# One-hot rows of four tokens as two pairs, one reduction over index candidates, and a GpSimd subtraction in pieces, in a two-layer decoder trunk

## The chip, the cores and the metric

The kernel runs on one core of one Trainium2 chip. The metric is the time of one execution on the device in microseconds (us), as the median of several runs. A profile is one further execution of the same program, recorded by the hardware profiler. Engine names are those of the profile: PE is TensorE's matmul, PEld its weight load, DVE is VectorE, ACT is ScalarE, POOL is GpSimd, SP is SyncE, whose queue issues most loads.

## What is computed

The reference is a decoder trunk of two layers on 256 tokens of width 1024. Each layer is a pair of token mixers (a gated linear recurrence and a stick-breaking attention) and then a PEER feed-forward block, which is where the change lies:

```
q = (h @ w_pq).reshape(B, S, 8 heads, 2, 64)
s1, s2 = q[..., 0, :] . sub_keys[0], q[..., 1, :] . sub_keys[1]     # 128 scores each
v1, i1 = top_k(s1, 16);  v2, i2 = top_k(s2, 16)
cand     = v1[:, None] + v2[None, :]                                # 256 candidates
cand_idx = i1[:, None] * 128 + i2[None, :]
top, pos = top_k(cand, 16);  idx = take_along_axis(cand_idx, pos)
gates    = softmax(top)
out      = sum over (head, k) of gates * gelu(h . peer_u[idx]) * peer_v[idx]
```

There are 128 x 128 = 16,384 experts, 8 heads and 16 experts a head, so 128 chosen experts per token.

## The kernel before

The kernel does not gather rows of `peer_u`. It computes the products of all experts with all tokens, multiplies them by a matrix of gates that is zero except at the chosen experts, and multiplies the result by all of `peer_v`. Everything is float32 in accuracy: each matmul operand is split into a rounded half `wh` and a remainder `wl`, and three matmuls (high by high, high by low, low by high) make one product.

**Loads and their preparation.** A list `order` holds all weight loads in the order of their use. `fetch` (line 179) issues the next one on SP into one of five `raw` buffers. A load of `peer_u` is one tile of 128 x 1024 in four DMAs (line 191). `turn` (line 209) transposes a `peer_u` tile in 32 x 32 blocks on DVE (line 214, `raw<-raw`). `prep` (line 221) makes the halves of a tile in two steps of 512 columns: ACT copies `raw` into `wh` (through `act`, line 58), and the remainder `wl = raw - wh` is a subtraction (line 254). For `peer_u` it is GpSimd's, with the columns taken in an order of blocks (`p a k r`); for other weights DVE or GpSimd does it. `take` (line 285) hands over a prepared tile, issues the next load, prepares the next tile and transposes the one after.

**The stage of `peer_u`** (lines 1302 to 1630) goes over 128 tiles, 126 of them in one loop (line 1622). Each `u_tile` (line 1605) issues 24 matmuls of 256 columns into the bank `A`: all 256 tokens against one tile. Every second tile, `fin_u` (line 1592) applies the gelu (ACT, tile `gel`) and, where the gates of a token are already in place, multiplies on DVE (line 1600).

After each tile the loop calls `pull(sides, 1.55)` (line 618), which runs a generator of side work: every step yields a cost, `pull` goes on until the budget of the tile is spent, and `yield None` ends the work for this tile. So the code's order on each engine is fixed at build time by these costs. The side work is:

- `topk` (line 1338): the two top-16 searches of every head and token block on DVE, with a small matmul for the scores (bank `K`).
- its second part (lines 1429 to 1477), which turns positions into indices. For each of the two token blocks and the two key halves `a`, it compares 16 positions with 16 candidates (`m`, 8 heads x 16 x 16 = 2048 values of float16, line 1449), multiplies by the candidates' indices (line 1453), and adds over the 16 candidates by halving: 1024, 512, 256 values (line 1458) and a last addition of 128 (line 1460). Two transposes per block go to PE (line 1469).
- `place_gates` (line 1480): for each block `b` of `TB` = 4 tokens, `build` makes one-hot rows. `o` is 1 where a key number equals a chosen index (line 1486), for both key halves; `og` is the row of the second half times the gate, itself in two float16 halves (line 1488). Both are tiles `[128, 2, 128 keys, 4 tokens]` of float16, 1024 values a partition, with the token innermost. `prod` then makes the gates of each token as `o`'s first half times `og`, eight matmuls of 128 columns per block (bank `G`, line 1497), with the weights `o[:, 0, :, q]` and the moving columns `og[:, a, :, q]`. Both are read with a step of four values, that is 8 bytes. `put` copies `G` out (ACT, and DVE at line 1512). The matmuls of block `b - 1` are issued ahead of the building of block `b`, and the copies behind it. There are 64 blocks a layer.

On each engine the order in a tile with gates is therefore: PE 24 matmuls `A`, then 8 matmuls `G`; DVE the transpose of a later `peer_u` tile, every second tile the multiplication by the gelu, the two operations of `build`, the multiplications of `put`; POOL the two subtractions of the next tile, each behind ACT's copy; ACT the copies of `put`, which wait for `G`, then the copies `wh` of the next tile.

**The stage of `peer_v`** (lines 1691 to 1718) has no part in the change.

Of the kernel before, what the change touches and what calls it, by code (L numbers as in the profile page):

```python
# [8 lines left out]
F32 = mybir.dt.float32  # L9
F32R = mybir.dt.float32r  # L10
F16 = mybir.dt.float16
# [5 lines left out]
P = 128  # L17
# [28 lines left out]
def trunk_kernel(ctx: ExitStack, tc: tile.TileContext, x, c, w_ada, b_ada, w_in, lb_logits, hg_norm_g,  # L46
# [174 lines left out]
    def prep():  # L221


        turn(1)
        kind, t = fetched[0]
        kind = kind[0]
        if kind in "mk":
            fetched.popleft()
            prepped.append((kind, t, None, None))
            return True  # L230
        place = room_for(kind)
        if not place:
            return False
        fetched.popleft()
        live.append(place)
        hs, ls = [], []
        if kind == "v" and state.get("vprep"):
            state["vprep"]()
        for s in range(2):
            h = place.tile([P, 512], F32R, name="wh")  # L240
            lo = place.tile([P, 512], F32R, name="wl")
            hs.append(h)
            ls.append(lo)
            if kind == "u":
                src = t.rearrange("p (a k r) -> p a k r", a=4, k=KC)[:, :, 4 * s:4 * s + 4]
                h, lo = (a.rearrange("p (k a r) -> p a k r", k=4, a=4) for a in (h, lo))
            else:
                src = t[:, s * 512:(s + 1) * 512]
            act(h, src, AF.Copy)
            if kind == "u" or state.get("pool_lo"):  # L250
                eng = nc.vector if s and state.get("share_lo") else nc.gpsimd
            else:
                eng = lighter(0.6, 1.0) if kind == "o" or kind == "w" and not state.get("slab") else nc.vector
            eng.tensor_sub(lo, src, h.bitcast(F32))  # L254
        h, lo = halves(hs), halves(ls)
        prepped.append((kind, h, lo, place))
        return True
# [50 lines left out]
        return prepped[0][0] if prepped else fetched[0][0][0] if fetched else None  # L308


    iota_t = const.tile([P, NK, TB], F16, name="iota_t")
    iota_k = const.tile([P, TOPK, TOPK], F16, name="iota_k")
    nc.gpsimd.tensor_copy(iota_t, iota_f[:, :, None].to_broadcast([P, NK, TB]))
    nc.gpsimd.tensor_copy(iota_k, iota_f[:, :TOPK, None].to_broadcast([P, TOPK, TOPK]))
    cols = const.tile([P, P], F32, name="cols")
    lncols = const.tile([P, 2, DEPTH, 2, KC], F32, name="lncols")
# [985 lines left out]
    def peer(l, hT):  # L1302
        with ExitStack() as es:
# [8 lines left out]
            with ExitStack() as eu:  # L1312
# [13 lines left out]
                def per_head(a):  # L1326
                    return a.rearrange("p (h k) -> p h k", h=PH)
# [10 lines left out]
                def topk():  # L1338
# [90 lines left out]
                    for tt in range(2):  # L1429
# [14 lines left out]
                        for a in range(2):  # L1444
                            iv = per_head(half[2 + a])[:, :, :, None].to_broadcast(k4)
                            for q in range(0, PH, 4):
                                act(ix[:, q:q + 4], iv[:, q:q + 4], AF.Copy)
                                yield None
                            nc.vector.tensor_tensor(m, per_head(half[a])[:, :, None, :].to_broadcast(k4),
                                                    iota_k[:, None].to_broadcast(k4), op=OP.is_equal)  # L1450
                            yield 1.1
                            yield None
                            nc.vector.tensor_mul(m, m, ix)
                            yield 1.1
                            w = TOPK
                            while w > 2:
                                w //= 2
                                nc.vector.tensor_add(m[:, :, :w], m[:, :, :w], m[:, :, w:2 * w])  # L1458
                                yield 0.3
                            nc.vector.tensor_add(per_head(sel[a]), m[:, :, 0], m[:, :, 1])  # L1460
                            yield 0.2
                        nc.vector.tensor_reduce(sm[:, :PH], tp, axis=mybir.AxisListType.X, op=OP.add)
                        nc.vector.reciprocal(sm[:, :PH], sm[:, :PH])
                        nc.vector.tensor_mul(tp, tp, sm[:, :PH][:, :, None].to_broadcast([P, PH, TOPK]))
# [15 lines left out]
                def place_gates():  # L1480

                    def build(b):
                        bs = slice(b * TB, (b + 1) * TB)
                        o = up.tile([P, 2, NK, TB], F16, name="o2", bufs=2)
                        og = up.tile([P, 2, NK, TB], F16, name="o3", bufs=3)
                        nc.vector.tensor_tensor(o, iT[:, :, None, bs].to_broadcast([P, 2, NK, TB]),  # L1486
                                                iota_t[:, None].to_broadcast([P, 2, NK, TB]), op=OP.is_equal)
                        nc.vector.tensor_mul(og, gT[:, :, None, bs].to_broadcast([P, 2, NK, TB]),  # L1488
                                             o[:, 1:2].to_broadcast([P, 2, NK, TB]))
                        built[b] = o, og  # L1490

                    def prod(b):
                        pg = psk.tile([P, TB, NK], F32, name="G")
                        o, og = built.pop(b)
                        for q in range(TB):
                            for a in range(2):
                                mm(pg[:, q], o[:, 0, :, q], og[:, a, :, q], a == 0, a == 1)
                        return pg

                    def put(b, pg):  # L1500
                        jd = progress["j"]
                        ts = slice(b * TB, (b + 1) * TB)
                        i = jd // NB_J
                        if jd < NK:
                            act(buf[i][:, jd % NB_J:, ts], pg[:, :, jd:(i + 1) * NB_J].rearrange("p t j -> p j t"), AF.Copy)
                        for i2 in range(i + 1, NK // NB_J):
                            act(buf[i2][:, :, ts], pg[:, :, i2 * NB_J:(i2 + 1) * NB_J].rearrange("p t j -> p j t"), AF.Copy)
                        for i2 in range(0, min(i + 1, NK // NB_J)):
                            n = min(jd - i2 * NB_J, NB_J)
                            if n > 0:  # L1510
                                dst = buf[i2][:, :n, ts]
                                nc.vector.tensor_mul(dst, pg[:, :, i2 * NB_J:i2 * NB_J + n].rearrange("p t j -> p j t"), dst)
                        progress["t"] = (b + 1) * TB

                    built, prods = {}, {}
                    nb = S // TB
                    for b in range(nb + 1):
                        if 0 <= b - 1 < nb:
                            prods[b - 1] = prod(b - 1)
                        if b < nb:  # L1520
                            build(b)
                        yield 1.2
                        if 0 <= b - 1 < nb:
                            put(b - 1, prods.pop(b - 1))

                        yield 0.1 + 0.2 * progress["j"] / NB_J
                        yield None
# [238 lines left out]
```

## Time and profile before

| | us |
|---|---|
| median of 3 runs | 2266.94 |
| the 3 runs | 2264.68, 2266.94, 2272.71 |
| the profiled execution, own time | 2268.03 |
| its span, first to last instruction | 2266.3 |
| granted TensorE clock, mean of the profiled execution | 0.979 |
| `peer_u` stage of layer 0, first to last | about 320 to 785 |
| `peer_u` stage of layer 1 | about 1435 to 1897 |

Start times are counted from the span's start. A group's row in the profile reads: line, engine, operation, output<-inputs, shapes, xcount | busy us, mean ns of one | idle time just before them and what ended it. "Busy" includes the time in which an instruction has been started and is held up. A row of the windows view reads: window, its length, then busy time and instruction count for PE, PEld, DVE, ACT and POOL, the granted clock, the DMA share and GB/s. A row of the chain of waits or of the timeline begins with start and length in us.

### The profile page before, as it was taken

The page shows a single profiled execution, that of the slowest core. Times are in us where ns is not written, and L with a number is a line of the kernel's source. Part 1 is how long each engine was busy: PE and PEld are TensorE (multiplying, and loading weights), DVE is VectorE, ACT ScalarE, POOL GpSimd, SP SyncE. Part 2 cuts the span into 40 slices and gives each one's busy share as a digit, 9 for nine tenths or more (in the row PEclk, how much of TensorE's full clock was granted, in tenths as well). Part 3 has the DMA queues.
Part 4 walks back from the last instruction along what each step waited for, and adds up shares of the span by engine and source line. Part 5 has one row for each costly group of instructions (what it writes and reads, how often), then busy time and mean ns, then how long its engine had stood idle before and what let it go on. Part 6 is the DMA issues. An engine that isn't in the chain of part 4 may idle for free.

```text
span 2266.3 us, 41171 instructions
## 1 busy us (share of the span) xinstructions
PE 2142.0 (95%) x14084; PEld 1951.7 (86%) x14084; DVE 1899.3 (84%) x3480; ACT 1116.2 (49%) x2347; POOL 1047.4 (46%) x760
## 2 busy tenths in 40 slices
PE   5789899899999999999989998998999999999998
PEld 5789799889999978888779897998999998788886
DVE  7877989999999878888887558999999997666675
ACT  3446544544444454555545564445444445455562
POOL 4656648786777610000045534687767773200001
PEclk8999999999999999999999999999999999999999
DMA  8546556555555578888844335564555555666672
GB/s 280 187 139 224 156 142 172 147 135 144 141 142 139 159 251 263 284 280 287 291 136 149 112 123 139 156 170 133 139 141 143 144 139 176 203 194 193 195 224 92
DMA packets 269515, 400.24 MB, mean 177 GB/s; under 512 B 29776, under 2 KB 216696, under 8 KB 269304
## 3 DMA queue, kind: packets, MB, share of 16 engines
q1 hardware_dynamic: 267560, 392.33, 57.3%
q0 software_dynamic: 1408, 4.23, 0.5%
q8 instruction: 110, 1.80, 0.3%
q10 hardware_dynamic: 336, 1.06, 0.1%
q14 instruction: 101, 0.83, 0.1%
HBM read 396.46 MB, written 1.05 MB: 175 GB/s over the span
## 4 chain that ended last, share of the span: by engine, by line
PE 70%; DVE 14%; DMA 5%; issue 4%; POOL 3%; ACT 2%; SPq 1%; POOLq 0%; DVEq 0%; ACTq 0%
PE Y L61 27%; PE A L61 25%; PE T L61 7%; PE G L61 6%; POOL wl L254 3%; DMA raw<-in_peer_u_dram 3%; PE hs L61 2%; PE ss L61 2%; DVE wl L254 2%; SPq L191 1%; DVE qk L840 1%; DVE e L826 1%; DMA raw<-in_peer_v_dram 1%; DVE mh L364 1%; DVE buf L1458 1%
## 5 line engine op out<-in xcount | busy, mean ns | idle before, releaser
L254 POOL TENSOR_TENSOR wl<-raw,wh 128x512 fp32r<-128x512 f32 x663 | 918.9, 1410 | 707.8 <-ACT wh L58 642.5
L58 ACT ACTIVATE wh<-raw 128x512 fp32r<-128x512 f32 x1188 | 682.7, 622 | 206.8 <-PE A L61 48.0
L61 PE MATMUL A<-hTh,wh 128*128 128x256 f32 x2080 | 545.3, 294 | 8.4 <-ACT wh L58 8.4
L61 PE MATMUL A<-hTl,wh 128*128 128x256 f32 x2080 | 528.0, 286 | 0.0
L61 PE MATMUL Y<-wh,o 128*128 128x512 f32 x1776 | 479.9, 392 | 0.1
L254 DVE TENSOR_TENSOR wl<-raw,wh 128x512 fp32r<-128x512 f32 x525 | 382.9, 770 | 62.0 <-ACT wh L58 43.5
L61 PEld LDWEIGHTS A<-hTh,wh 128*128 128x128 f32 x2080 | 405.1, 195 | 10.3 <-ACT wh L58 9.3
L61 PEld LDWEIGHTS A<-hTl,wh 128*128 128x128 f32 x2080 | 403.6, 194 | 0.8
L61 PEld LDWEIGHTS Y<-wh,o 128*128 128x128 f32 x1776 | 334.6, 189 | 69.8 <-ACT wh L58 0.8
L61 PE MATMUL A<-hTh,wl 128*128 128x256 f32 x2080 | 341.6, 287 | 8.0 <-POOL wl L254 7.5
L214 DVE STREAM_TRANSPOSE raw<-raw 128x1024 f32<-128x1024 f32 x256 | 312.5, 1229 | 0.2
L61 PEld LDWEIGHTS A<-hTh,wl 128*128 128x128 f32 x2080 | 290.9, 194 | 14.2 <-POOL wl L254 14.1
L61 PE MATMUL Y<-wl,o 128*128 128x512 f32 x888 | 277.0, 393 | 9.4 <-DVE wl L254 9.4
L58 ACT ACTIVATE o<-buf 128x256 fp32r<-128x256 f32 x228 | 95.0, 417 | 281.1 <-PE Y L61 281.0
L504 DVE TENSOR_TENSOR o<-buf,o 128x256 fp32r<-128x256 f32 x228 | 99.7, 437 | 148.6 <-ACT o L58 148.6
L61 PEld LDWEIGHTS Y<-wl,o 128*128 128x128 f32 x888 | 168.0, 189 | 47.7 <-DVE wl L254 12.7
L58 ACT ACTIVATE buf<-G 128x128 f32<-128x128 f32 (+15 forms) x248 | 51.5, 257 | 267.0 <-PE G L61 267.0
L61 PE MATMUL G<-o,o 128*128 128x128 f16 x1024 | 142.0, 296 | 5.5 <-DVE o L1488 5.5
L553 POOL TENSOR_TENSOR x<-x,buf 128x1024 f32<-128x1024 f32 x1 | 2.4, 2398 | 290.8 <-DVE x L550 290.8
L61 PE MATMUL T<-hTh,wh 128*128 128x256 f32 x512 | 133.5, 293 | 0.0
L1486 DVE TENSOR_TENSOR o<-iT,iota_t 128x1024 f16<-128x1024 f16 x128 | 131.6, 1028 | 0.0
L61 PE MATMUL T<-hTl,wh 128*128 128x256 f32 x512 | 130.0, 286 | 0.0
(493 smaller groups left out, 3130.9 us busy)
## 6 DMA issues: line engine op xcount, KB each, us to landing
raw<-in_peer_u_dram SPq DMA_DIRECT2D x1024, 128.0 KB, 3.3
raw<-in_peer_v_dram SPq DMA_DIRECT2D x256, 512.0 KB, 4.3
raw<-in_w_in_dram SPq DMA_DIRECT2D x88, 512.0 KB, 4.5
raw<-in_w_ada_dram SPq DMA_DIRECT2D x78, 512.0 KB, 4.7
raw<-in_w_o_dram SPq DMA_DIRECT2D x16, 512.0 KB, 3.4
raw<-in_w_pq_dram SPq DMA_DIRECT2D x64, 128.0 KB, 3.1
qk<-in_w_ada_dram SPq DMA_DIRECT2D x10, 512.0 KB, 3.6
e<-in_w_ada_dram SPq DMA_DIRECT2D x8, 512.0 KB, 6.1
```

The lines of the kernel that those rows point to most:

```text
L58: nc.scalar.activation(o, i, f, **kw)
L61: nc.tensor.matmul(o, a, b, start=start, stop=stop, **kw)
L191: nc.sync.dma_start(dst[32 * b:32 * b + 32], src[b])
L214: nc.vector.transpose(t, t)
L254: eng.tensor_sub(lo, src, h.bitcast(F32))
L364: nc.vector.scalar_tensor_tensor(acc, w, cond[:, k:k + 1], acc, op0=OP.mult, op1=OP.add)
L504: nc.vector.tensor_sub(lo, src, h.bitcast(F32))
L553: nc.gpsimd.tensor_mul(xt[tt], xt[tt], last[0])
L826: eng.tensor_sub(ev[:, :, :hn], mid, bv[:, :, :hn])
L840: nc.vector.tensor_mul(tv[:, :, hn:], nodes(qT, n)[:, :, hn:], ev[:, :, hn:])
L1458: nc.vector.tensor_add(m[:, :, :w], m[:, :, :w], m[:, :, w:2 * w])
L1486: nc.vector.tensor_tensor(o, iT[:, :, None, bs].to_broadcast([P, 2, NK, TB]), iota_t[:, None].to_broadcast([P, 2, NK, TB]), op=OP.is_equal)
```

## The change

1. GpSimd's subtraction for `peer_u` (line 254) is issued as two instructions, each over two of the four blocks `k`, that is 256 columns instead of 512. A tile has four such instructions instead of two. Other weights are as before.
2. The four additions by halving (lines 1455 to 1461) become one `tensor_reduce` over the 16 candidates. It reads the 2048 float16 values with the candidate innermost, which is a step of 16 values, or 32 bytes, and writes 128 float32 values. Its cost for `pull` is 1.4 in one step, instead of 0.3 + 0.3 + 0.3 + 0.2 in four.
3. The one-hot tiles become `[128, 2, 2 pairs, 128 keys, 2 tokens]`. Each of the two operations of `build` is issued as two of 512 values. In `prod` the weights and the moving columns are read with a step of two values, 4 bytes. The table `iota_t` has two copies of each key number instead of four.

```
-            eng.tensor_sub(lo, src, h.bitcast(F32))
+            if kind == "u" and eng is nc.gpsimd:
+
+                for k in range(0, 4, 2):
+                    eng.tensor_sub(lo[:, :, k:k + 2], src[:, :, k:k + 2], h.bitcast(F32)[:, :, k:k + 2])
+            else:
+                eng.tensor_sub(lo, src, h.bitcast(F32))
...
-                            w = TOPK
-                            while w > 2:
-                                w //= 2
-                                nc.vector.tensor_add(m[:, :, :w], m[:, :, :w], m[:, :, w:2 * w])
-                                yield 0.3
-                            nc.vector.tensor_add(per_head(sel[a]), m[:, :, 0], m[:, :, 1])
-                            yield 0.2
+                            nc.vector.tensor_reduce(per_head(sel[a]), m.rearrange("p h a k -> p h k a"),
+                                                    axis=mybir.AxisListType.X, op=OP.add)
+                            yield 1.4
...
-                        o = up.tile([P, 2, NK, TB], F16, name="o2", bufs=2)
-                        og = up.tile([P, 2, NK, TB], F16, name="o3", bufs=3)
-                        nc.vector.tensor_tensor(o, iT[:, :, None, bs].to_broadcast([P, 2, NK, TB]),
-                                                iota_t[:, None].to_broadcast([P, 2, NK, TB]), op=OP.is_equal)
-                        nc.vector.tensor_mul(og, gT[:, :, None, bs].to_broadcast([P, 2, NK, TB]),
-                                             o[:, 1:2].to_broadcast([P, 2, NK, TB]))
+
+                        pairs = [P, 2, TB // 2, NK, 2]
+                        o = up.tile(pairs, F16, name="o2", bufs=2)
+                        og = up.tile(pairs, F16, name="o3", bufs=3)
+                        for u in range(TB // 2):
+                            us = slice(b * TB + 2 * u, b * TB + 2 * u + 2)
+                            nc.vector.tensor_tensor(o[:, :, u], iT[:, :, None, us].to_broadcast([P, 2, NK, 2]),
+                                                    iota_t[:, None].to_broadcast([P, 2, NK, 2]), op=OP.is_equal)
+                        for u in range(TB // 2):
+                            us = slice(b * TB + 2 * u, b * TB + 2 * u + 2)
+                            nc.vector.tensor_mul(og[:, :, u], gT[:, :, None, us].to_broadcast([P, 2, NK, 2]),
+                                                 o[:, 1:2, u].to_broadcast([P, 2, NK, 2]))
...
-                                mm(pg[:, q], o[:, 0, :, q], og[:, a, :, q], a == 0, a == 1)
+                                mm(pg[:, q], o[:, 0, q // 2, :, q % 2], og[:, a, q // 2, :, q % 2], a == 0, a == 1)
```

More of the change, by code (lines that the diff above doesn't have):

```diff
@@ L308, in next_kind @@
         return prepped[0][0] if prepped else fetched[0][0][0] if fetched else None
-    iota_t = const.tile([P, NK, TB], F16, name="iota_t")
+    iota_t = const.tile([P, NK, 2], F16, name="iota_t")
     iota_k = const.tile([P, TOPK, TOPK], F16, name="iota_k")
-    nc.gpsimd.tensor_copy(iota_t, iota_f[:, :, None].to_broadcast([P, NK, TB]))
+    nc.gpsimd.tensor_copy(iota_t, iota_f[:, :, None].to_broadcast([P, NK, 2]))
     nc.gpsimd.tensor_copy(iota_k, iota_f[:, :TOPK, None].to_broadcast([P, TOPK, TOPK]))
```

## Prediction

> **What bounds the kernel now.** The page first: PE is busy 95% of the span, and the chain that ended last is PE's for 70%.
>
> ```profile
> span 2266.3 us, 41171 instructions
> PE 70%; DVE 14%; DMA 5%; issue 4%; POOL 3%; ACT 2%; SPq 1%; POOLq 0%; DVEq 0%; ACTq 0%
> ```
>
> Then the windows view over the parts of the `peer_u` stage: top-k, selection, gates, and top-k and selection of layer 1.
>
> ```profile
> 320.00:428.00 108.00, 105.28 (x842) 104.24 (x841) 107.56 (x461) 54.77 (x104) 84.11 (x67) 0.98 0.60 164
> 428.00:484.00 56.00, 46.91 (x340) 42.82 (x338) 55.14 (x57) 27.46 (x44) 46.99 (x30) 0.97 0.50 135
> 500.00:600.00 100.00, 100.00 (x839) 98.62 (x838) 97.65 (x150) 47.02 (x141) 70.73 (x54) 1.00 0.51 142
> 1536.00:1597.00 61.00, 51.75 (x366) 47.65 (x367) 60.07 (x66) 30.10 (x49) 49.96 (x32) 0.95 0.48 130
> ```
>
> Two regimes. In the selection DVE is full and PE loses 56 - 46.91 = 9.1 us in layer 0 and 61 - 51.75 = 9.25 us in layer 1: 18.3 us that a lighter DVE could give back. With gates PE has no gap, and DVE is full as well (97.65 of 100). The timeline of one tile with gates shows why; the last DVE row is the next tile's first.
>
> ```profile
> 574.76 0.68 DVE L1486 TENSOR_TENSOR o<-iT,iota_t 128x1024 f16<-128x1024 f16 x1
> 575.48 0.69 DVE L1488 TENSOR_TENSOR o<-gT,o 128x1024 f16<-128x1024 f16 x1
> 576.09 0.57 DVE L1512 TENSOR_TENSOR buf<-G,buf 128x128 f32<-128x128 f32 x3
> 576.57 1.24 DVE L214 STREAM_TRANSPOSE raw<-raw 128x1024 f32<-128x1024 f32 x1
> 577.73 1.40 DVE L1486 TENSOR_TENSOR o<-iT,iota_t 128x1024 f16<-128x1024 f16 x1
> ```
> ```profile
> 572.11 2.55 POOL L254 TENSOR_TENSOR wl<-raw,wh 128x512 fp32r<-128x512 f32 x2 [1.19 <-ACT wh L58]
> 575.93 2.65 POOL L254 TENSOR_TENSOR wl<-raw,wh 128x512 fp32r<-128x512 f32 x2 [1.28 <-ACT wh L58]
> ```
>
> The second comparison took 1.40 us where the first took 0.68: it started at 577.73 and finished 0.55 us after POOL's pair ended (575.93 + 2.65 = 578.58). So a DVE operation with two inputs in SBUF and a GpSimd subtraction exclude each other, each holding the other up for a whole instruction. POOL's period is 575.93 - 572.11 = 3.82 us: 2.55 of POOL, then a gap of 1.27 into which DVE's pair (574.76 to 576.09, 1.33) just fits. The gates stage is bounded by PE, with this exchange hardly behind it.
>
> PE's own 3.82 us come from the chain of waits:
>
> ```profile
> 494.55 0.94 PE G L61 x8
> 495.50 2.86 PE A L61 x24
> ```
>
> A tile is 24 matmuls, a block of gates 8: 2.86 + 0.94, and about 0.02 of switching.
>
> **The change, part by part.**
>
> *The reduction* takes away four additions per unit (a token block and a key half; four units a layer, eight in all). Rows of the selection in layer 0 (four units), two other reductions of DVE, and one operation that reads short runs:
>
> ```profile
> L1458 DVE TENSOR_TENSOR buf<-buf 128x1024 f16<-128x1024 f16 (+2 forms) x12 | 17.3, 1438 | 0.4
> L1460 DVE TENSOR_TENSOR buf<-buf 128x128 f32<-128x128 f16 x4 | 5.0, 1246 | 0.1
> L1462 DVE TENSOR_REDUCE buf<-buf 128x8 f32<-128x128 f32 x2 | 0.5, 274 | 0.0
> ```
> ```profile
> L376 DVE TENSOR_REDUCE mod<-A 128x4 f32<-128x512 f32 x20 | 13.7, 683 | 0.3 <-PE A L369 0.3
> ```
> ```profile
> L870 DVE COPY_PREDICATED sc<-masks,hs x16: 422/439/749, 125.1 to 1273.6; 128x256 f32<-128x256 uint8 x14, 128x512 f32<-128x512 uint8 x2
> ```
>
> Removed: (17.3 + 5.0) / 4 = 5.6 us per unit, nearly all of it waiting, since even 128 values take 1.25 us: each addition waits for one subtraction. Added: a reduction of 2048 values. From 128 to 512 values it costs (683 - 274) / 384 = 1.07 ns a value, so 683 + 1536 x 1.07 = 2.3 us; it has one input, so I take it that it waits for nobody. That is the low end. It reads with steps of 32 bytes; the row with short runs goes from 422 to 749 ns at 256 values, 1.28 ns more a value, which gives 2.3 + 2.6 = 4.9 us as the high end. I take 2.3 to 3.5, nearer to the rows of the same operation. Per layer DVE is then lighter by 4 x (5.6 - 2.3) = 13 us at most, 55.1 to 42 in layer 0 and 60.1 to 47 in layer 1, below PE's 46.9 and 51.75: PE becomes the bound and the gain is capped by its 18.3 us. At 3.5 us DVE comes out at 46.7 and 51.7, level with PE. Two engines that are level don't overlap fully, so I book -13 of the 18. At 4.9 us DVE falls by 4 x 0.7 = 2.8 a layer, -5 in all: bounds -5 to -18. The new `pull` costs (1.4 for 1.1) add 4 x 0.3 = 1.2 to a layer's budget of 1.55 a tile, so the gates start less than a tile later; five tiles without gates follow the last block and take that up:
>
> ```profile
> 770.18 14.40 PE A L61 x120
> ```
>
> [...]
>
> *The step of the one-hot rows, on PE.* Rows for 256 and 512 moving columns, and weight loads:
>
> ```profile
> 784.58 46.28 PE Y L61 x204
> ```
> ```profile
> L61 PEld LDWEIGHTS A<-hTl,wh 128*128 128x128 f32 x2080 | 403.6, 194 | 0.8
> L61 PEld LDWEIGHTS <-o 128*128 128x128 f16 x1024 | 103.8, 118 | 13.5 <-DVE o L1488 7.1
> ```
> ```profile
> L61 PEld LDWEIGHTS A<-sb_w,v_b 128*64 128x64 f32 x64 | 7.3, 136 | 5.4 <-DVE obl L504 1.1 <-issue 0.2
> ```
>
> 512 columns take 46.28 / 204 = 0.227 us, 256 take 2.86 / 24 = 0.119: 0.42 ns a column and 0.011 fixed, so 128 columns should take 0.065. `G` takes 0.94 / 8 = 0.118, just what 256 columns take. The weights aren't it: 64 columns less of float32 save 58 ns of load, and the float16 load, at 118 against 194, is 76 ns shorter still. So the moving columns, 8 bytes apart, come at half rate. At 4 bytes, the step of the float32 rows, I expect the full rate: 8 x 0.053 = 0.42 us less a block, and 1024 / 8 = 128 blocks: 54 us of PE time. Bounds: nothing, and -54.
>
> [...]
>
> *DVE and POOL in the gates stage* decide how much of it is seen. The comparison's durations (min/median/max):
>
> ```profile
> L1486 DVE TENSOR_TENSOR o<-iT,iota_t x128: 640/680/1809, 489.8 to 1879.8; 128x1024 f16<-128x1024 f16 x128
> ```
>
> An operation of 1024 values takes 0.64 us at the least, too little for one value per 1.07 ns, so two go at a time: 512 x 1.07 = 0.55 and 0.09 fixed. One of 512 values should take 0.27 + 0.09 = 0.36, and four 1.4 us, for 1.33 now. The first `og` operation waits for `o`, as before.
>
> ```profile
> L553 POOL TENSOR_TENSOR x<-x,buf 128x1024 f32<-128x1024 f32 x1 | 2.4, 2398 | 290.8 <-DVE x L550 290.8
> ```
> ```profile
> 2261.45 1.03 POOL L563 TENSOR_TENSOR x<-x,buf 128x256 f32<-128x256 f32 x1 [4.54 <-DVE x L562]
> 2262.55 0.92 POOL L564 TENSOR_TENSOR x<-x,buf 128x256 f32<-128x256 f32 x1
> ```
>
> POOL's 1024 columns take 2.40, 512 half of 2.55: 1.12 per 512, so a piece of 256 takes 1.28 - 0.56 = 0.72, of which 0.56 is reading; beside DVE work the two rows show 0.92 and 1.03. Four pieces are 2.9 us a tile for 2.55. One after the other, POOL and DVE need 2.9 + 1.4 = 4.3 us; with every piece and every DVE operation alternating without loss, 4 x (0.56 + 0.27) = 3.3. PE would need 3.82 - 0.42 = 3.40. The middle of the two exchanges is 3.8, today's period. I therefore book nothing, with bounds from 3.40 (-54) to 4.3 (+0.48 x 128 = +61).
>
> *The rest* I cost at nothing. Top-k: POOL's 67 subtractions become 134 x 0.72 = 96 of 108 us; without that room each tile would pay the excess over PE. Behind a tile's last piece on POOL's queue stands only the next tile's first, which waits for ACT anyway; SP's next load waits for the `raw` buffer 0.35 us longer, against a ring of five tiles of over 3 us; uncovered, that would be 0.35 x 252 = 88 us. Behind DVE's operations stand `put`'s multiplications and the next transpose, and PE's next `G` waits for `og`: that is rival 3. The smaller `iota_t` lies ahead of everything.
>
> **Sum.** Against the profiled execution's 2268.0: -13 + 0 = 2255; the median of the runs shown is 1.1 lower, so 2254.
>
> **The rivals.** One more row, POOL in the gates window 500 to 600:
>
> ```profile
> L254 POOL TENSOR_TENSOR wl<-raw,wh 128x512 fp32r<-128x512 f32 x54 | 71.2, 1340 | 29.5 <-ACT wh L58 29.4
> ```
>
> 1. *Forecast, 0.40.* Selection -13, gates within 8 us of today: 2246 to 2262.
> 2. *PE's gain comes through, 0.22.* DVE waits shrink with the pieces, and the period goes to 3.6 or below: -0.2 x 128 = -26 with -13: 2228, at the extreme 2254 - 54 = 2200. For it: 29.4 us of POOL's idle time per 100 us end with ACT, not with DVE. Against it: DVE has no idle time to give.
> 3. *The exchange becomes the bound, 0.26.* POOL's longer run (2.9) leaves a gap of 0.9, too short for DVE's 1.4 us, so two of the four operations fall among the pieces and wait 0.5 us each; DVE falls behind until `G` waits for `og`. At 4.05 us: +0.23 x 128 = +29: 2283. It decides from 3.92 on, where 0.1 x 128 eats the selection's gain.
> 4. *Neither read gets faster, 0.12.* The reduction costs 4.9 us and `G` stays at 0.94: -5, and some loss: 2255 to 2270, 2264 in the middle. For it: nothing in the trace shows either new read at its full rate. Against it: the half rate of `G` has no other cause in the rows. [...]
>
> **How the numbers follow.** Time: the likeliest case, 2254. Range: 2224 takes in most of case 2, 2285 most of case 3; case 1 alone is 2246 to 2262. A measurement can tell some 0.3%, 6.8 us, from no change, so faster is below 2260. Faster: nearly all of 1 (0.31), all of 2, a sixth of 4 (0.02): 0.54 with rounding down. Slower, above 2273.7: most of 3 (0.23) and a little of 4: 0.24. The rest, 0.22, is the same.
>
> **What would show it.** The reduction's row near 2.3 to 3.5 us, and PE busy in the selection windows near their length; `G` at 0.5 us a block in the chain; `L254` pieces at a mean of 0.75 to 0.9; DVE still full with gates and the period near 3.8. The prediction is wrong if `G` stays at 0.94, if the reduction takes 5 us, or if PE shows waits for DVE's `o` in the hundreds of ns a block.

## The result, and the profile after

The changed kernel takes 2300.39 us (median of 4 runs, 2299.04 to 2303.76), the kernel before in the same comparison 2266.53 (4 runs): a ratio of 1.0145, 95% interval 1.0128 to 1.0161. It is slower by some 34 us. Forecast were 2254, with a range up to 2285. The profiled execution took 2299.04 us.

The head of the profile's page, with the span and the shares of the chain that ended last:

```profile
span 2297.2 us, 42432 instructions
...
PE 40%; DVE 13%; POOL 12%; DMA 7%; issue 5%; SPq 2%; ACT 1%; POOLq 0%; DVEq 0%; ACTq 0%
```

This chain is followed back to 443 us only and its shares add up to 80%, so PE's 40% can't be set beside the 70% of before as it stands. Over the same stretch, 500 to 780 us, the two chains do compare: before, PE's matmuls `A` and `G` carry 69% and 19% of it, now 17% and 3%; GpSimd's subtraction carried 3% and now carries 28%, the loads of `peer_u` under 1% and now 12%. The windows view, first the selection and then two stretches with gates (columns as in the prediction's rows: PE, PEld, DVE, ACT, POOL, clock, DMA share, GB/s):

```profile
430.00:493.00 63.00, 57.72 (x447) 54.28 (x445) 62.49 (x60) 31.86 (x54) 60.09 (x73) 1.00 0.52 151
500.00:600.00 100.00, 91.12 (x800) 85.28 (x798) 99.16 (x186) 46.95 (x135) 81.72 (x103) 1.00 0.47 138
600.00:700.00 100.00, 89.06 (x755) 82.11 (x753) 97.47 (x184) 41.43 (x108) 80.03 (x100) 1.00 0.44 128
```

With gates PE was busy 100.00 of 100 before; now it is idle for 9 to 11 us of each 100, while DVE is as full as it was. The selection did get lighter: PE loses 63 - 57.72 = 5.3 us there, for 9.1 of 56 before. The groups of the changed operations, from the source views of the reduction and of the second product, then from the page's groups of GpSimd's pieces:

```profile
L1460 DVE TENSOR_REDUCE buf<-buf x8: 4060/4122/4139, 434.4 to 1603.0; 128x128 f32<-128x2048 f16 x8
```
```profile
L1495 DVE TENSOR_TENSOR o<-gT,o x256: 407/950/1001, 488.6 to 1920.7; 128x512 f16<-128x512 f16 x128
...
  PE G L61: 53.7, 108
  PEld L61: 39.1, 50
```
```profile
L257 POOL TENSOR_TENSOR wl<-raw,wh 128x256 fp32r<-128x256 f32 x1024 | 807.2, 823 | 175.6 <-ACT wh L58 148.7
```

The `og` operation takes 0.41 us when nothing holds it up and 0.95 in the middle of its 256 executions, and PE's `G` waited for it 53.7 us in all. The timeline shows how, DVE first and then POOL, over nearly the same stretch as in the prediction:

```profile
572.80 0.71 DVE L1491 TENSOR_TENSOR o<-iT,iota_t 128x512 f16<-128x512 f16 x2
573.43 1.33 DVE L1495 TENSOR_TENSOR o<-gT,o 128x512 f16<-128x512 f16 x2
574.68 0.56 DVE L1519 TENSOR_TENSOR buf<-G,buf 128x128 f32<-128x128 f32 x3
575.17 1.23 DVE L214 STREAM_TRANSPOSE raw<-raw 128x1024 f32<-128x1024 f32 x1
576.33 0.59 DVE L1607 TENSOR_TENSOR buf<-buf,gel 128x160 f32<-128x160 f32 x1
576.85 0.75 DVE L1491 TENSOR_TENSOR o<-iT,iota_t 128x512 f16<-128x512 f16 x2
577.52 1.83 DVE L1495 TENSOR_TENSOR o<-gT,o 128x512 f16<-128x512 f16 x2
579.27 0.57 DVE L1519 TENSOR_TENSOR buf<-G,buf 128x128 f32<-128x128 f32 x3
579.77 1.23 DVE L214 STREAM_TRANSPOSE raw<-raw 128x1024 f32<-128x1024 f32 x1
580.92 0.71 DVE L1491 TENSOR_TENSOR o<-iT,iota_t 128x512 f16<-128x512 f16 x2
```
```profile
573.74 3.01 POOL L257 TENSOR_TENSOR wl<-raw,wh 128x256 fp32r<-128x256 f32 x4 [1.21 <-ACT wh L58]
577.27 3.37 POOL L257 TENSOR_TENSOR wl<-raw,wh 128x256 fp32r<-128x256 f32 x4 [0.52 <-ACT wh L58]
```

From 572.80 to 580.92 are two tiles: 4.06 us each, for 3.82 before. The two comparisons (0.71 and 0.75 for the pair) run free. GpSimd then starts its four pieces, at 573.74 and 577.27, and the two products of each tile take 1.33 and 1.83 us, where two free ones take 2 x 0.41: one of the two waits in the first tile, both in the second. In some tiles it is worse. Here all four operations wait, beside a GpSimd run of eight pieces, those of two tiles, and the two lines that took 0.71 and 1.33 above take 3.6 us:

```profile
756.39 1.83 DVE L1491 TENSOR_TENSOR o<-iT,iota_t 128x512 f16<-128x512 f16 x2
758.14 1.81 DVE L1495 TENSOR_TENSOR o<-gT,o 128x512 f16<-128x512 f16 x2
```
```profile
754.55 6.69 POOL L257 TENSOR_TENSOR wl<-raw,wh 128x256 fp32r<-128x256 f32 x8 [1.53 <-ACT wh L58]
```

Over both layers, 280 of the 512 operations last at least 0.2 us longer than a free one of 0.41 us, 2.2 of four in a block, and about as many late in a stage as early. The gates stage of layer 0, from its first comparison to its last, ran from 489.81 to 767.03 us before and runs from 487.28 to 790.43 us now. That is 277 us and 303 us; with layer 1 (277 and 304) the gates take 53 us more. The rest of the kernel gives some 19 of them back.

### The profile page after: what moved, and what is told of

Its sections match the earlier page's. It is cut to its first block, busy times and chain, and to the rows that moved or that the text cites. A ratio compares the mean times of both kernels' runs of the same rounds, so it can differ in the third digit from the quotient of the medians.

```text
span 2297.2 us, 42432 instructions
## 1 busy us (share of the span) xinstructions
PE 2119.9 (92%) x14084; PEld 1900.1 (83%) x14084; DVE 1940.5 (84%) x3716; ACT 1121.3 (49%) x2339; POOL 1146.3 (50%) x1272
## 4 chain that ended last, share of the span: by engine, by line
PE 40%; DVE 13%; POOL 12%; DMA 7%; issue 5%; SPq 2%; ACT 1%; POOLq 0%; DVEq 0%; ACTq 0%
PE Y L61 27%; POOL wl L257 12%; DMA raw<-in_peer_u_dram 6%; PE A L61 6%; PE T L61 4%; SPq L191 2%; DVE raw L214 2%; DVE o L1495 2%; DVE wl L259 1%; DVE o L1491 1%; PE G L61 1%; PE hs L61 1%; PE ss L61 1%; DVE buf L1519 1%; DMA raw<-in_peer_v_dram 1%
## 5 line engine op out<-in xcount | busy, mean ns | idle before, releaser
L257 POOL TENSOR_TENSOR wl<-raw,wh 128x256 fp32r<-128x256 f32 x1024 | 807.2, 823 | 175.6 <-ACT wh L58 148.7
L259 POOL TENSOR_TENSOR wl<-raw,wh 128x512 fp32r<-128x512 f32 x151 | 211.2, 1421 | 466.0 <-ACT wh L58 452.1
L61 PEld LDWEIGHTS A<-hTh,wh 128*128 128x128 f32 x2080 | 400.5, 193 | 19.3 <-ACT wh L58 18.3
L61 PE MATMUL A<-hTh,wl 128*128 128x256 f32 x2080 | 361.2, 290 | 16.9 <-POOL wl L257 13.7
L61 PEld LDWEIGHTS A<-hTh,wl 128*128 128x128 f32 x2080 | 295.8, 193 | 36.1 <-POOL wl L257 33.7
L1495 DVE TENSOR_TENSOR o<-gT,o 128x512 f16<-128x512 f16 x256 | 208.6, 853 | 0.0
L61 PE MATMUL G<-o,o 128*128 128x128 f16 x1024 | 95.3, 220 | 54.3 <-DVE o L1495 53.7
L58 ACT ACTIVATE buf<-G 128x128 f32<-128x128 f32 (+14 forms) x240 | 50.0, 256 | 187.8 <-PE G L61 187.8
```

What stands on the lines that cost most here:

```text
L58: nc.scalar.activation(o, i, f, **kw)
L61: nc.tensor.matmul(o, a, b, start=start, stop=stop, **kw)
L257: eng.tensor_sub(lo[:, :, k:k + 2], src[:, :, k:k + 2], h.bitcast(F32)[:, :, k:k + 2])
L1495: nc.vector.tensor_mul(og[:, :, u], gT[:, :, None, us].to_broadcast([P, 2, NK, 2]), o[:, 1:2, u].to_broadcast([P, 2, NK, 2]))
```

## The experiments

### The parts alone, and the layout without the split

The first theory (the "exchange" of the expectations): PE's gain is real, but four DVE operations and four GpSimd pieces that exclude each other make DVE the bound. Its rivals: the pieces alone are the loss (one), the splitting of DVE's operations alone is (two), the reduction carries a part of it (three).

`pieces_only` is the kernel before with change 1 alone.

> The kernel before with GpSimd's pieces of 256 columns alone. Theory (exchange): in the gates stage DVE and GpSimd hold each other up, and the loss comes from four pieces of GpSimd meeting four operations of DVE. With only two DVE operations a tile, the period grows from 3.82 by the longer run of GpSimd alone, 0.1 to 0.25 us on 128 blocks: 2279 to 2299. Rival one (the pieces are the whole loss): 2300 or more. Rival two (the splitting of DVE's operations is the whole loss): 2267, no change.

Measured: 2260.94 us, ratio 0.9957 (0.9943 to 0.9972). All three expectations missed: the pieces are a gain. This gain lies ahead of the gates, whose first comparison starts at 484.17 us for 489.81 before; in the window 500 to 600 PE is busy 100.00 of 100, as before.

`reduce_only` is the kernel before with change 2 alone.

> The kernel before with the one reduction alone. The reduction took 4.1 us in the changed kernel for 5.6 us of additions. Theory: the selection shortens by about 2.5 us a layer and nothing else moves: 2261 to 2264, at the edge of what can be told. Rival three (the reduction carries a part of the loss, as its pull cost of 1.4 moves the gates later): 2270 or more.

Measured: 2260.28, ratio 0.9961 (0.9949 to 0.9972). That is just under the theory's 2261 to 2264, and rival three fell: the reduction is a gain as well, some 9 us.

`pairs_only` is the kernel before with change 3 alone.

> The kernel before with the pair layout alone, so four DVE operations of 512 values a block and GpSimd in 512 columns. Theory (exchange): the G matmuls take 0.47 us a block, and the period is set by DVE and GpSimd: 2.55 + 1.4 with some overlap, 3.7 to 3.9 for 3.82: 2252 to 2277. Rival one (the pieces are the whole loss): PE's gain comes through, 3.5 or less: below 2230. Rival two (the splitting of DVE's operations is the whole loss): 2300.

Measured: 2372.47, ratio 1.0454 (1.0437 to 1.0472). None of the three expectations reached that far; rival two, at 2300, had the cause but a third of the size. The whole loss is in change 3, some 100 us of it, and with the other two changes a third is left.

`merged_no_pieces` has changes 2 and 3, but makes `o` and `og` with one instruction of 1024 values each. So that one instruction can cover both pairs, the tiles are laid out pair first, and `iT` and `gT` hold two tokens of each half side by side; `G` reads at 4 bytes as in the changed kernel.

```
+                        pairs = [P, TB // 2, 2, NK, 2]
+                        nc.vector.tensor_tensor(o.rearrange("p u a k t -> p (u a) k t"), ...)
+                        nc.vector.tensor_mul(og, ...)
...
+                                mm(pg[:, q], o[:, q // 2, 0, :, q % 2], og[:, q // 2, a, :, q % 2], a == 0, a == 1)
```

> The changed kernel with GpSimd in 512 columns again, and with the token pair as the outer dimension of the index and gate tables, so that the pair layout needs one DVE operation of 1024 values for o and one for og, as before the change. Theory (exchange): G takes 0.47 us a block and DVE has two operations; the period falls to 3.55 to 3.75: 2235 to 2255, and faster than pairs_only. If the number of DVE operations did not matter, it would equal pairs_only less the reduction's 5 us.

Measured: 2294.23, ratio 1.0118 (1.0092 to 1.0144). This missed: two DVE operations and 512 columns are what the kernel before has, and yet the loss was there. Its timeline, DVE and then POOL:

```profile
567.28 1.78 DVE L1486 TENSOR_TENSOR o<-iT,iota_t 128x1024 f16<-128x1024 f16 x1
569.10 1.63 DVE L1489 TENSOR_TENSOR o<-gT,o 128x1024 f16<-128x1024 f16 x1
...
572.30 0.64 DVE L1486 TENSOR_TENSOR o<-iT,iota_t 128x1024 f16<-128x1024 f16 x1
572.98 0.69 DVE L1489 TENSOR_TENSOR o<-gT,o 128x1024 f16<-128x1024 f16 x1
```
```profile
567.20 2.98 POOL L254 TENSOR_TENSOR wl<-raw,wh 128x512 fp32r<-128x512 f32 x2
573.16 2.92 POOL L254 TENSOR_TENSOR wl<-raw,wh 128x512 fp32r<-128x512 f32 x2 [2.98 <-ACT wh L58]
```

In one tile both operations meet a GpSimd run, each waits about 1 us, and the next pair starts 572.30 - 567.28 = 5.02 us later; in the next tile neither waits. So I made a second theory, "pace": PE, at 3.82 us a tile, was the slowest engine and so set when GpSimd runs; a faster PE lets GpSimd's run drift onto DVE's pair.

### Is it PE's pace, the order, or the exclusion at all?

`double_g` is the changed kernel with PE made slow again.

```
+                        for r in range(2):
                             for q in range(TB):
                                 for a in range(2):
                                     mm(pg[:, q], ...)
```

> The changed kernel with every block's eight G matmuls issued twice; the second pass starts its sums anew, so the gates are the same and PE's work per block is back near the 0.94 us of the kernel before (16 x 0.058 = 0.93), while DVE and GpSimd have exactly the instructions of the changed kernel. Theory (pace): PE at 0.118 a matmul was the slowest engine and set when ACT and GpSimd run; a faster PE hands the pace to DVE, and GpSimd's run then falls on DVE's pair. With PE slow again the period returns to 3.8 to 3.9 us, the gates windows show PE full, and the time is 2250 to 2275. Rival (count): four DVE operations and four pieces a tile cost the exchange more than two and two, whoever sets the pace. Then PE's added work of 0.46 us lies in PE's waits at best, the period stays at 4.05 or rises, and the time is 2300 or more.

Measured: 2301.59, ratio 1.0145 (1.0119 to 1.0172), just as the changed kernel and as the rival (count) had it. Pace fell, for this kernel. Its windows:

```profile
500.00:600.00 100.00, 98.38 (x1001) 96.47 (x1001) 99.16 (x190) 45.72 (x136) 81.83 (x104) 1.00 0.47 138
600.00:700.00 100.00, 93.59 (x918) 90.41 (x917) 97.49 (x184) 41.25 (x108) 80.01 (x99) 1.00 0.44 130
```

PE's extra work went into its idle time, and DVE and POOL show the busy time of the changed kernel within 0.2 us: those two set the rhythm here.

`turn_early` moves one DVE instruction of the changed kernel.

```
-        turn(1 if kind == "u" else 3)
+        turn(2 if kind == "u" else 3)
```

> The changed kernel with DVE's transpose of a peer_u tile issued one tile earlier (turn(2) for turn(1)). Theory (ring): in the changed kernel ACT's copy starts some 0.15 us after the transpose that DVE issues just before its pair, so GpSimd's run always meets DVE's products. With a tile of slack behind the transpose ACT and GpSimd can run ahead of DVE, the period falls to 3.6 to 3.9 and the time to 2235 to 2275. Rival (sum): GpSimd's 2.9 us of pieces and DVE's 1.3 to 1.4 us exclude each other wherever they stand, so that the period is 4.05 or more with any order: 2295 to 2305.

Measured: 2382.43, ratio 1.0513 (1.0479 to 1.0547). Both theories missed. The timeline of DVE, then POOL:

```profile
575.79 1.84 DVE L1491 TENSOR_TENSOR o<-iT,iota_t 128x512 f16<-128x512 f16 x2
577.55 1.81 DVE L1495 TENSOR_TENSOR o<-gT,o 128x512 f16<-128x512 f16 x2
```
```profile
575.74 3.34 POOL L257 TENSOR_TENSOR wl<-raw,wh 128x256 fp32r<-128x256 f32 x4 [1.79 <-ACT wh L58]
```

ACT and GpSimd did get ahead of DVE, and so the run starts together with DVE's first comparison instead of its first product: all four operations of this tile wait now, 0.5 us each. Over both layers 429 of the 512 wait, for 280 in the changed kernel. So the order matters, and starting GpSimd's run earlier in this way gives it no room.

`no_sub_pairs` and `no_sub_quads` leave out GpSimd's subtraction for `peer_u`; the matmuls that read `wl` read `wh` instead. The first has changes 2 and 3, the second only change 2.

```
-            lo = place.tile([P, 512], F32R, name="wl")
+            lo = h if kind == "u" else place.tile([P, 512], F32R, name="wl")
```

> The changed kernel without GpSimd's subtraction for peer_u: the two matmuls of a product that read the remainder read the rounded half instead, so PE, DVE and ACT have the work of the changed kernel and nothing on GpSimd excludes DVE. Both forms of the theory: the exclusion is what hides PE's gain, so the gates run at PE's 2.9 + 0.5 = 3.4 us a tile, about 250 us of gates stage for 300, and with a lighter top-k and selection the time is 2170 to 2200. Rival (DVE's own work or the lower clock is the bound): the period stays at 3.8 or above, 2230 or more.

> The same without GpSimd's subtraction for peer_u, with the reduction but with the one-hot rows as in the kernel before: the control for the run on pairs. PE is the bound there with 2.86 + 0.94 = 3.82 us a tile, so the gates stage stays at about 273 us. If G's half rate is real work of PE, this run is 40 to 54 us slower than the one on pairs: 2220 to 2245. If both come out alike, PE's gain never was one.

Measured: 2158.29 (2 runs, ratio 0.9516, 0.9484 to 0.9548) and 2213.74 (2 runs, 0.976, 0.9726 to 0.9794). The chain of waits of the first, then of the second; both are PE's alone there:

```profile
522.42 2.92 PE A L61 x24
525.34 0.48 PE G L61 x8
```
```profile
502.29 0.95 PE G L61 x8
```

Both are faster than expected, by 12 and by 6 us. PE's gain is real: 0.95 - 0.48 = 0.47 us a block, 60 us for 128 blocks, of which 55.5 us show between the two runs. So what hides it lies in GpSimd's subtraction. Whether that is the exclusion or the subtraction's own 3 us a tile, these two runs don't separate, since they leave out both.

The same two kernels give the price of DVE's operations without GpSimd. The windows view of the tile `o` alone counts, in its DVE column, the time in which DVE works on `o` and `og`; this is its sum over the gates stages of both layers, pairs first:

```profile
sum 502.00, PE 79.88 PEld 57.87 DVE 180.11 ACT 0.00; mean PE 39.94 PEld 28.93 DVE 90.06 ACT 0.00
```
```profile
sum 552.00, PE 139.56 PEld 102.21 DVE 174.01 ACT 0.00; mean PE 69.78 PEld 51.11 DVE 87.00 ACT 0.00
```

Over 128 blocks that is 1.41 us a block for four operations and 1.36 for two. By themselves four cost DVE hardly more than two: 6 us in the whole kernel.

### Number of operations, or layout?

The third theory, "number of waits": each DVE operation that meets GpSimd's run waits for the rest of one GpSimd instruction, so the price is the number of DVE operations times the length of a GpSimd instruction. By it, splitting GpSimd's halves the price of each wait, and splitting DVE's doubles their number.

`no_pairs` is the kernel before with changes 1 and 2.

> The kernel before with GpSimd's pieces and the reduction, without the pair layout. Each alone brought it to 0.996. If they work in different places (pieces in the selection and in the gates, the reduction in the selection and in the order of the steps behind it) the two add up: 2248 to 2254, ratio 0.990 to 0.993. If both only fill the same idle time of PE in the selection, the second adds nothing: 2258 to 2262.

Measured: 2257.78, ratio 0.9948 (0.9931 to 0.9965). That is at the edge of the second expectation: on top of the pieces the reduction adds little.

`merged_pieces` is `merged_no_pieces` with GpSimd's pieces, that is the changed kernel with two DVE operations a block for four.

> The changed kernel with o and og each made by one DVE instruction of 1024 values in the pair layout (two locked operations a block for four), GpSimd in pieces, G at 0.058 us. Theory (number of waits): every DVE operation with two inputs in SBUF that meets a GpSimd run waits for the rest of one GpSimd instruction, so the price is the number of DVE operations times the length of a GpSimd instruction. With two operations and pieces the waits are at most 2 x 0.55 us, the period is 3.6 to 3.85 and the time 2235 to 2257. Rival (pace): a PE that needs only 3.40 us a tile makes DVE the slowest engine, whatever the number of operations; then this run loses as the merged one without pieces did: 2280 to 2300.

Measured: 2253.97, ratio 0.9936 (0.9914 to 0.9958), as number of waits had it. It beats the kernel before and the changed one; from `no_pairs` the intervals don't separate it.

`merged_double` is `merged_no_pieces` with the second pass of `G` that `double_g` has.

> The pair layout with one DVE instruction each for o and og, GpSimd in 512 columns, the reduction, and every block's eight G matmuls issued twice, so that PE needs 0.94 us a block again. Without the second pass this kernel took 2294. Pace: with PE slow again it comes back to the kernel with the reduction alone, which differs from it only in the layout: 2255 to 2268, gates stage 278 us. Number of waits: PE's pace has no part in it, 2290 or more.

Measured: 2266.18, ratio 0.9978 (0.9965 to 0.999), against 1.0118 without the second pass. A kernel with eight more matmuls a block is the faster one: for two long operations against two long subtractions, pace holds, and number of waits, with its 2290 or more, missed. Its window shows PE gap-free, as before:

```profile
500.00:600.00 100.00, 100.00 (x1033) 98.92 (x1032) 98.38 (x148) 45.78 (x137) 69.07 (x54) 1.00 0.52 143
```

`og_quads` is the changed kernel with `og` in the old layout, still written by two instructions.

```
-                        og = up.tile(pairs, F16, name="o3", bufs=3)
+                        og = up.tile([P, 2, NK, 2, 2], F16, name="o3", bufs=3)
...
-                            nc.vector.tensor_mul(og[:, :, u], ...)
+                            nc.vector.tensor_mul(og[:, :, :, u], ...)
...
-                                mm(pg[:, q], o[:, 0, q // 2, :, q % 2], og[:, a, q // 2, :, q % 2], a == 0, a == 1)
+                                mm(pg[:, q], o[:, 0, q // 2, :, q % 2], og[:, a, :, q // 2, q % 2], a == 0, a == 1)
```

> The changed kernel with og written as two instructions into the old layout (moving columns of G at a step of 8 bytes), o in pairs (weights at 4 bytes). If the moving columns alone cause G's half rate, G is back at 0.118 us a matmul; if the weights have a part in it, it is in between. For the time, number of waits: four DVE operations as in the changed kernel, so 2295 to 2305 although PE is slow. Pace: 2250 to 2275.

Measured: 2302.06 (2 runs), ratio 1.0145 (1.0117 to 1.0172). Eight matmuls `G` in its timeline, then in that of `no_sub_pairs` (the last one's end is included):

```profile
566.60 1.09 PE L61 MATMUL G<-o,o 128*128 128x128 f16 x8
```
```profile
568.35 0.63 PE L61 MATMUL G<-o,o 128*128 128x128 f16 x8
```

With the weights at 4 bytes and the moving columns at 8, `G` is slow again: the moving columns are enough to make the half rate. And the time is the changed kernel's, though PE gained nothing: the loss isn't in `G`'s speed but in DVE's four operations.

`three_ops` and `four_ops` are `merged_pieces` with the same tiles, but with `og`, or both `o` and `og`, made by one instruction for each pair. The lines show `og`; `four_ops` does the same with `o`.

```
-                        nc.vector.tensor_mul(og, gT[:, bs][:, :, :, None].to_broadcast(pairs), ...)
+                        for u in range(TB // 2):
+                            nc.vector.tensor_mul(og[:, u], gT[:, bs][:, u, :, None].to_broadcast(...), ...)
```

> The pair layout with pieces and reduction; o is one DVE instruction of 1024 values, og two of 512 (three locked operations a block; with two the time was 2254, and the changed kernel has four). Number of waits: each further operation meets one more GpSimd piece and waits some 0.55 us in most tiles, so this run lies between the two, 2268 to 2290. Rival (layout: the order in which pairs and key halves lie in the tiles, not the number of instructions, made the merged kernel fast): this run stays at 2250 to 2260.

> The same tiles as in the kernel with one instruction each for o and og, but two instructions of 512 values each: only the number of DVE instructions is that of the changed kernel, not the order in its tiles. Number of waits: 2293 to 2305. Layout: 2250 to 2260.

Measured: 2290.13, ratio 1.0092 (1.0077 to 1.0108), and 2304.08, ratio 1.016 (1.0145 to 1.0175). Number of waits held: 2290.13 lies at the very top of its 2268 to 2290, 2304.08 within its 2293 to 2305. Layout fell. The same windows view of the tile `o` over the gates stages of both layers, of `merged_pieces`, `three_ops`, `four_ops` and `turn_early`:

```profile
sum 570.00, PE 80.55 PEld 58.55 DVE 269.09 ACT 0.00; mean PE 40.28 PEld 29.28 DVE 134.55 ACT 0.00
```
```profile
sum 601.00, PE 94.42 PEld 62.24 DVE 305.55 ACT 0.00; mean PE 47.21 PEld 31.12 DVE 152.77 ACT 0.00
```
```profile
sum 616.00, PE 95.10 PEld 62.48 DVE 331.19 ACT 0.00; mean PE 47.55 PEld 31.24 DVE 165.59 ACT 0.00
```
```profile
sum 687.00, PE 96.27 PEld 64.49 DVE 409.17 ACT 0.00; mean PE 48.13 PEld 32.25 DVE 204.58 ACT 0.00
```

In the table an operation counts as waiting when it lasts at least 0.2 us longer than a free one (0.41 us, or 0.68 for 1024 values):

| kernel | operations a block | waiting, of all | DVE on `o` and `og`, us | time, us |
|---|---|---|---|---|
| `merged_pieces` | 2 | 206 of 256 | 269 | 2253.97 |
| `three_ops` | 3 | 245 of 384 | 306 | 2290.13 |
| `four_ops` | 4 | 280 of 512 | 331 | 2304.08 |
| `turn_early` | 4 | 429 of 512 | 409 | 2382.43 |

From row to row DVE's time rises by 36, 26 and 78 us, and the kernel's by 36, 14 and 78. Without GpSimd four operations took 6 us more than two; beside its pieces they take 62 us more. So the waits account for the times, to within some 12 us. Their number grows with the operations but doesn't double from two to four, since not every operation meets GpSimd's run.

### The reduction's read

`flat_reduce` is `merged_pieces` with the comparison `m` laid out so that the candidate is innermost.

```
-                            iv = per_head(half[2 + a])[:, :, :, None].to_broadcast(k4)
+                            iv = per_head(half[2 + a])[:, :, None, :].to_broadcast(k4)
...
-                            nc.vector.tensor_tensor(m, per_head(half[a])[:, :, None, :].to_broadcast(k4),
+                            nc.vector.tensor_tensor(m, per_head(half[a])[:, :, :, None].to_broadcast(k4),
...
-                            nc.vector.tensor_reduce(per_head(sel[a]), m.rearrange("p h a k -> p h k a"),
+                            nc.vector.tensor_reduce(per_head(sel[a]), m,
```

> The pair layout with one instruction each for o and og, pieces, and the reduction with the comparison laid out with the candidate innermost, so that the reduction reads its 2048 float16 values one after the other instead of at a step of 32 bytes. If the step is what made the reduction cost 4.12 us, it now takes 2.1 to 2.6 us, DVE is 4 x 1.6 = 6 us lighter a layer in the selection (less if the comparison reads slower with its repeated operand innermost), and since PE can take only some 4 us of it a layer the time is 2244 to 2251. Rival (a reduction of float16 into float32 costs 2 ns a value however it reads): 4.0 to 4.2 us, and 2252 to 2257 as without the edit.

Measured: 2260.55, ratio 0.9965 (0.9953 to 0.9977). The reduction and the comparison in the source views, of `flat_reduce` and then of `merged_pieces`:

```profile
L1460 DVE TENSOR_REDUCE buf<-buf x8: 2286/2286/2287, 436.0 to 1586.3; 128x128 f32<-128x2048 f16 x8
...
L1454 DVE TENSOR_TENSOR buf<-buf,iota_k x8: 2244/2404/2775, 431.4 to 1581.5; 128x2048 f16<-128x2048 f16 x8
```
```profile
L1454 DVE TENSOR_TENSOR buf<-buf,iota_k x8: 1175/1704/1761, 430.8 to 1574.7; 128x2048 f16<-128x2048 f16 x8
```

The step does make the reduction's price: 2.29 us for 4.12. But the comparison, whose repeated operand now stands innermost, goes from 1.18 us at the least to 2.24. For the time, both expectations missed: the kernel comes out some 0.3% slower than `merged_pieces`, at the edge of what the intervals separate. The comparison doesn't explain that, since DVE's work on the two together is still less: 18.9 us in the selection of layer 0, for 22.7 in `merged_pieces`. What the trace shows is that DVE is no longer full there. It now waits for loads of `peer_u` in the selection of layer 0, where it had no such wait in `merged_pieces`; the row is from the groups in the window 430 to 491:

```profile
L214 DVE STREAM_TRANSPOSE raw<-raw 128x1024 f32<-128x1024 f32 x19 | 22.9, 1226 | 3.9 <-DMA raw<-in_peer_u_dram 3.9
```

Why the loads come late, no run shows.

## Why the prediction was wrong

**PE's step was right.** 0.42 us a block were to go; the chain of `no_sub_pairs` shows 0.48 a block for 0.95. `og_quads` shows that the moving columns alone are enough to bring the half rate back: 1.09 us for eight matmuls there, 0.63 in `no_sub_pairs`, the end of the last included.

**The reduction was mis-sized.** Expected were 2.3 to 3.5 us, measured 4.12, within the prediction's bounds of 2.3 to 4.9. The low end was the price of reading in order (2.29 in `flat_reduce`), and I leaned to it because the reduction row in the prediction was of the same operation. The step of the read costs 1.8 us on top. The row behind the high end was misread: its 749 ns are of 512 values, and of the executions with 256 ten take 0.42 to 0.45 us and four 0.73 to 0.74, so it doesn't show 1.28 ns a value for short runs. The part alone still brought 9 of the 13 us: a unit is 5.6 - 4.12 = 1.5 us lighter, 12 us in eight units. That it waits for nobody held: its eight executions lie within 0.08 us. One input alone, the prediction's reason, doesn't make it so: a cast of the kernel before has one input too, and takes 0.21 us in six of its eight executions and 1.32 in the two that start within a GpSimd subtraction:

```profile
L1435 DVE CAST buf<-buf x8: 211/215/1315, 424.5 to 1570.5; 128x128 f16<-128x128 uint32 x8
```

**The failed step is the gates stage**: "The middle of the two exchanges is 3.8, today's period. I therefore book nothing". The single prices were right: four operations take 1.39 us without GpSimd (571.13 to 571.77 + 0.75 in the rows of `no_sub_pairs` below; forecast 1.4), a piece 0.823 in the mean (forecast 0.75 to 0.9). Wrong was to take the middle between no overlap, 4.3 us a tile, and lossless alternation, 3.3, and so to book the gates at nothing: they cost 53 us. A layer's gates have 73 tiles before and 74 now, 3.80 and 4.10 us each in the mean, nearer to no overlap than to the middle. The two engines don't alternate without loss. A DVE operation that meets GpSimd's run waits some 0.5 us for the rest of a piece (275 of the 280 that wait end 0.25 to 0.3 us after the piece in which they start), and it holds up the next one: a piece takes 0.74 us from 575.31 on, beside a transpose, and 0.91 to 0.93 in three of the four from 577.27 on, beside the two products. Where the run starts decides how many of the four meet it: one at 573, two at 577, all four at 756, 2.2 in the mean, and 3.4 in the mean of `turn_early`. `put`'s multiplications, with one input in the bank `G`, and the transposes don't wait for it: in the changed kernel 348 of 398 and 188 of 256 start while a subtraction runs, and the longest take 0.28 and 1.26 us, as the rows behind the pair show.

```profile
571.13 0.72 DVE L1490 TENSOR_TENSOR o<-iT,iota_t 128x512 f16<-128x512 f16 x2
571.77 0.75 DVE L1494 TENSOR_TENSOR o<-gT,o 128x512 f16<-128x512 f16 x2
```
```profile
L1519 DVE TENSOR_TENSOR buf<-G,buf x398: 148/274/280, 494.6 to 1924.0; 128x128 f32<-128x128 f32 x139, 128x80 f32<-128x80 f32 x6, 128x112 f32<-128x112 f32 x6, 128x88 f32<-128x88 f32 x5
...
L214 DVE STREAM_TRANSPOSE raw<-raw x256: 1191/1227/1256, 311.9 to 1922.3; 128x1024 f32<-128x1024 f32 x128
```

**Rival 3 is what happened**, with its mechanism: about two of the four wait 0.5 us each, the period is 4.06 in the two tiles shown (4.05 in the prediction), and `G` waits for `og`, 53.7 us in all or 0.42 us a block, which the prediction had named as a sign of being wrong. It was given 2283. What it missed is in its sum: it priced 128 blocks at 0.23 us, 29 us, where the gates stages of two layers have some 147 tiles, not every one with a block of its own. These became 0.30 us longer each in the mean, with one more tile a layer. And it put the loss down to GpSimd's longer run (2.9 us of pieces), when splitting GpSimd's instruction is a gain, beside four operations too (DVE's time on `o` and `og` is 404 us in `pairs_only` and 331 in the changed kernel), and the number of DVE's operations is the loss.

**Rival 2's condition** came out as its "against" said: DVE has no idle time to give. Without GpSimd's subtraction most of PE's gain comes through, 55.5 of 60 us. **Rival 4** fell: `G` did come down to half, and the reduction's 4.12 us lies below its 4.9.

**What stays open.** Why a run meets the products in one kernel and the comparisons in another is read from timelines (ACT's copies follow `put` and DVE's transpose) and wasn't tested beyond `turn_early`. Why pace decides with 512 columns and two operations, and not with pieces and four, is shown as a fact by `merged_double` and `double_g`; the drift that I give for it is only argued. A start of GpSimd's run behind DVE's pair wasn't tried. In `merged_pieces` PE's gain stays hidden too, with GpSimd busy 93.80 of 100 us; how much of that is the exclusion and how much the length of GpSimd's own run isn't separated. And the loads of `peer_u`, which the prediction costed at nothing, carry 12% of the changed kernel's chain from 500 to 780 us; they land in 3.1 us, as before, so they start later, but no run with more `raw` buffers shows whether they add to the loss.

## What to carry to other kernels

Where two engines exclude each other per instruction, price a split by waits: the number of instructions that meet the other engine's run, times what is left of one of its instructions (0.5 us for pieces of 256 columns here). As the runs of this kernel have it, split the engine whose instructions the full one waits for; don't split the full one's. And before a gain on one engine is booked, ask which other engine is full in the same stage: here `G` at half its price is worth 55 us without GpSimd's subtraction, and with it nothing that the intervals of `merged_pieces` and `no_pairs` can tell.

## What the runs showed of the hardware that was not expected

- Float16 moving columns at a step of 8 bytes run at half rate: eight matmuls of 128 columns take 0.95 us at 8 bytes and 0.48 at 4.
- A DVE comparison of 2048 float16 values takes 1.18 us at the least with the repeated operand in the middle and 2.24 with it innermost.
- A reduction of 2048 float16 values takes 2.29 us read in order and 4.12 at a step of 32 bytes, its eight executions within 0.08 us beside a busy GpSimd.
- More work on PE can make a kernel faster: `merged_double` takes 2266 us, and 2294 without its second pass.
